# First loads in halves, wide products ahead of narrow ones, copies ahead of ropes, last sparse heads one step on: four edits to a two-layer trunk

## The chip, the cores and the metric

The kernel runs on one core of a Trainium2 chip. The metric is device time in microseconds for one execution: load of inputs from memory, both layers, output back to memory. A profile gives the engines' instructions of one execution: TensorE (PE) with its weight loads (PEld), VectorE (DVE), ScalarE (ACT), GpSimd (POOL) and SyncE (SP), which here issues most loads.

## The reference, cut to what matters

```python
for i in range(DEPTH):                       # 2 layers, x is 256 x 1024, float32
    h = x @ w_in[i]                          # 1024 x 6214: q, k, v of three mixers, indexer, gates
    (fq, fk, fv, ff_logit, sq, sk, sv, dq, dk, dv, iq, ik, iw, g) = split_cols(h)
    log_f = log_sigmoid(ff_logit + b_forget[i])
    o_fox = fox_attention(fq, fk, fv, log_f)                     # 6 heads of 64
    o_sb = stick_breaking_attention(sq, sk, sv)                  # 5 heads
    dq, dk, iq, ik = rope(dq), rope(dk), rope(iq), rope(ik)
    o_dsa = dsa_attention(dq, dk, dv, iq, ik, iw)                # 5 heads, 64 keys chosen by an indexer
    gates = sigmoid(g.reshape(b, s, 3, D_MODEL))
    merged = (gates[:, :, 0] * (o_fox @ w_up_fox[i]) + gates[:, :, 1] * (o_sb @ w_up_sb[i])
              + gates[:, :, 2] * (o_dsa @ w_up_dsa[i]))
    x = layer_norm(ALPHA * x + merged @ w_out[i], ln1_g[i], ln1_b[i])
    ffn = square(relu(x @ w_ff_in[i])) @ w_ff_out[i]             # 1024 -> 4096 -> 1024
    ple = sigmoid(x @ w_ple_gate[i]) * (p[i] @ w_ple[i])         # p is 256 x 256 in each layer
    x = layer_norm(ALPHA * x + ffn + ple, ln2_g[i], ln2_b[i])
```

## The kernel before

**Products.** Every float32 product is made of three products in the format fp32r: a tile is split into a high part (`hi`, a cast on ScalarE) and a low part (`lo`, source minus high part, on VectorE), and high by high, high by low and low by high are added up in a PSUM bank. `split` (L178) does this, its cast at L181, its subtraction at L182. `wunit` (L206) loads a piece of a weight through SyncE's queue into one of five buffers (`wr`, 128x1024 at most, `wload` L95) and splits it into `wh` and `wl`, five buffers each. TensorE then multiplies. There are eight PSUM banks in two groups of four, `pg` and `ps`.

**Tiling.** The 256 tokens are two tiles of 128. `xstat` (L242) keeps the tokens' transposed tile as the stationary side and moves the weights, 512 columns at a time; `by_tile` (L251, L256) does one token tile's high products for all units, then its low ones, and then the second tile's. `wstat` (L399) keeps the weight stationary and moves the tokens, 256 columns (L407, L409, L410). `half_T` (L320) transposes half a token tile (L217) and splits it.

**The start.** p and the weights for p's embedding (`w_ple`, first half, two pieces of 128x512) are asked for first, then x's first tile, the first gate weight of 128x1024, x's second tile. `rope` and `bf` go on GpSimd's queue, behind which GpSimd makes the masks. p is transposed (L334) and split, its products (L197) fill two banks, x is transposed and split, and `gate(0)` is made by tile (`gate` L384): 48 products for the two tiles. `ple_done` (L338) copies p's two finished banks out on ScalarE (L341). The order on each engine comes from a scheduler, apart from a few instructions held in program order by `tc.keep_in_program_order`.

**The middle.** A planner (L863 on) lets one list of products (`PRODUCTS`, L31) and one list of jobs (`JOBS`, L32) run side by side: each step issues products until 550 columns are in flight (`PACE`) and one part of each job under way. The number beside a job's name is how many steps pass before the next job may start. The sparse heads are three jobs: `dsa0`, `dsa1` (heads 1 and 2) and `dsa3` (heads 3 and 4); their scores are made at L204 into `ps` banks, and `values` (L582) casts the values product of an earlier head out of such a bank (L592, L593). `c4_done` (L544) and `c3_done` (L552) take keys and values of the sparse and stick-breaking heads out of their bank: first `do_rope` (L364, VectorE pieces L369 to L373), then the `split` into `vh` and `vl`. `fv_done` (L429) adds the forget bias and splits v.

**The gated up products.** `up` (L812) multiplies the mixers' outputs by the up weights into pairs of `pg` banks (L197, L779, L780). The gates' sigmoid (L888) must come behind all exponentials of the layer, so its bias `zero` (L885) is computed from the last head's low part; then VectorE multiplies gate and bank (L762) and the bank is free for a later pair.

**The feed forward.** `ff_in` (L936) runs 16 times, over 512 of the hidden columns each, into four `ps` banks. Each has four units of two 128-row blocks with four banks each: a wide product (L945, 512 columns: high weight by high and low part of x side by side), and right behind it a narrow one (L947, 256 columns: low weight by high x). `ff_out` (L965) then adds 48 products of 512 columns to the layer's output.

## Time and profile before

| | us |
|---|---|
| median of three runs | 885.36 |
| the runs | 884.37, 885.36, 885.51 |
| profiled execution | 885.02 |
| its span | 883.3 |
| TensorE busy | 857.3 (97%) |
| VectorE busy | 642.1 (73%) |
| ScalarE busy | 476.0 (54%) |
| granted TensorE clock, mean | 0.993 |

The span is the time between the first and last instruction that the profile holds; 1.7 us of the profiled execution lie around it. The table says that TensorE works or stands in a queue of its own work nearly all the time. A product's record lasts longer than its place in the row, since products are pipelined: the spacing from start to start is what a run of products takes for each.

### The profile page before, as it was taken

Reading aid. Unit: us, or ns where it says so; the run is one execution under the profiler, and the core shown is the slowest. Engines: PE = TensorE matmul, PEld = TensorE weight load, DVE = VectorE, ACT = ScalarE, POOL = GpSimd, SP = SyncE. Lnnn points to the kernel's source line nnn. Section 1 sums busy time; section 2 is a strip of 40 time slices with the busy share of each in tenths; the row PEclk is TensorE's granted clock in tenths of the full one; section 3 lists DMA queues with packets and bytes.
Section 4 is the critical chain, followed back from the end, with each engine's and each line's share of the span. In section 5 each row is a group of like instructions: output and inputs, shape, how many; then the busy total and the mean of one; then the engine's idle time right before and its main releaser. Section 6 shows DMA issues by size and latency. Waiting matters only on the chain. (4 is left out here: it accounts for less than half of the span.)

```text
span 883.3 us, 12940 instructions
## 1 busy us (share of the span) xinstructions
PE 857.3 (97%) x4678; PEld 733.3 (83%) x4678; DVE 642.1 (73%) x1133; ACT 476.0 (54%) x749; POOL 71.2 (8%) x138
## 2 busy tenths in 40 slices
PE   5999999999999999999999999999999999999996
PEld 4999988788888888888879989787887888888885
DVE  5479997769877666666676889968797776666665
ACT  4445657667445444444354556666843654444440
POOL 2003111100011000000000121001001010000100
PEclk9999999999999999999999999999999999999998
DMA  8555666442656556666536646554364666666731
GB/s 264 167 151 138 178 193 172 158 148 97 211 179 229 191 190 191 191 213 215 174 91 192 170 135 197 160 182 153 111 228 152 214 191 191 191 188 189 235 127 48
DMA packets 79696, 154.46 MB, mean 175 GB/s; under 512 B 10096, under 2 KB 25456, under 8 KB 79632
## 3 DMA queue, kind: packets, MB, share of 16 engines
q1 hardware_dynamic: 77952, 149.04, 54.1%
q0 software_dynamic: 1680, 4.60, 1.8%
q8 instruction: 37, 0.61, 0.3%
q14 instruction: 27, 0.22, 0.1%
HBM read 152.30 MB, written 1.05 MB: 174 GB/s over the span
## 5 line engine op out<-in xcount | busy, mean ns | idle before, releaser
L182 DVE TENSOR_TENSOR wl<-wr,wh 128x1024 fp32r<-128x1024 f32 (+5 forms) x303 | 342.8, 1142 | 178.9 <-ACT wh L181 176.6
L181 ACT CAST wh<-wr 128x1024 fp32r<-128x1024 f32 (+5 forms) x303 | 295.2, 983 | 286.0 <-PE pg L197 110.2
L197 PE MATMUL pg<-wh,t16k 128*128 128x512 f32 (+4 forms) x768 | 224.7, 367 | 0.1
L945 PE MATMUL ps<-t16k,wh 128*128 128x512 f32 x512 | 181.4, 398 | 0.0
L197 PE MATMUL pg<-wh,t2k 128*128 128x512 f32 x544 | 172.8, 394 | 1.4 <-ACT wh L181 1.2
L197 PEld LDWEIGHTS pg<-wh,t16k 128*128 128x128 f32 x768 | 140.8, 189 | 20.0 <-DVE t2k L190 0.7
L947 PE MATMUL ps<-t16k,wl 128*128 128x256 f32 x512 | 143.7, 281 | 0.0
L197 PE MATMUL pg<-wl,t16k 128*128 128x512 f32 (+4 forms) x384 | 139.6, 364 | 0.0
L197 PEld LDWEIGHTS pg<-wh,t2k 128*128 128x128 f32 x544 | 102.9, 189 | 24.0 <-ACT wh L181 1.6
L945 PEld LDWEIGHTS ps<-t16k,wh 128*128 128x128 f32 x512 | 96.2, 188 | 23.8
L197 PE MATMUL pg<-wl,t2k 128*128 128x512 f32 x272 | 106.6, 392 | 0.0
L947 PEld LDWEIGHTS ps<-t16k,wl 128*128 128x128 f32 x512 | 96.7, 189 | 0.6
L197 PEld LDWEIGHTS pg<-wl,t16k 128*128 128x128 f32 x384 | 72.5, 189 | 8.3
L197 PEld LDWEIGHTS pg<-wl,t2k 128*128 128x128 f32 x272 | 51.6, 190 | 10.7 <-DVE wl L182 0.3
L407 PE MATMUL pg<-t16k,wh 128*128 128x256 f32 x176 | 50.5, 287 | 2.4 <-DVE t16k L182 2.4
L410 PE MATMUL pg<-t16k,wl 128*128 128x256 f32 x176 | 49.8, 283 | 0.0
L409 PE MATMUL pg<-t16k,wh 128*128 128x256 f32 x176 | 49.7, 283 | 0.0
L251 PE MATMUL pg<-wh,t16k 128*128 128x512 f32 x96 | 39.0, 406 | 4.8 <-ACT t16k L181 4.8
L251 PE MATMUL pg<-wl,t16k 128*128 128x512 f32 x96 | 38.6, 403 | 0.0
L197 PE MATMUL pg<-wh,t1k 128*128 128x512 f32 x112 | 37.3, 397 | 0.0
L407 PEld LDWEIGHTS pg<-t16k,wh 128*128 128x128 f32 x176 | 33.7, 191 | 2.9 <-issue 2.8
L409 PEld LDWEIGHTS pg<-t16k,wh 128*128 128x128 f32 x176 | 33.7, 191 | 0.0
(180 smaller groups left out, 968.9 us busy)
## 6 DMA issues: line engine op xcount, KB each, us to landing
wr<-in_w_ff_in_dram SPq DMA_DIRECT2D x64, 512.0 KB, 3.8
wr<-in_w_ff_out_dram SPq DMA_DIRECT2D x64, 512.0 KB, 3.5
wr<-in_w_in_dram SPq DMA_DIRECT2D x48, 512.0 KB, 4.1
wr<-in_w_in_dram SPq DMA_DIRECT2D x32, 384.0 KB, 3.6
wr<-in_w_out_dram SPq DMA_DIRECT2D x16, 512.0 KB, 3.7
wr<-in_w_ple_gate_dram SPq DMA_DIRECT2D x16, 512.0 KB, 5.2
wr<-in_w_in_dram SPq DMA_DIRECT2D x16, 256.0 KB, 2.9
wr<-in_w_in_dram SPq DMA_DIRECT2D x8, 390.0 KB, 3.7
```

Source lines behind the costliest of these rows:

```text
L181: a = nc.scalar.copy(hi, src)
L182: b = nc.vector.tensor_sub(lo, src, hi.bitcast(F32))
L197: nc.tensor.matmul(o, l, r, start=start and i == 0, stop=stop and i == 2, skip_group_check=skip)
L251: nc.tensor.matmul(o[t][:, :n], tok(aT, u * nk + kk, t)[0], wt[i][:, kk, :], start=u + kk + i == 0, stop=False)
L407: nc.tensor.matmul(oi, hi, rh, start=kb == 0 and i % 2 == 0, stop=False, skip_group_check=True)
L409: nc.tensor.matmul(oi, hi, rl, start=False, stop=False, skip_group_check=True)
L410: nc.tensor.matmul(oi, lo, rh, start=False, stop=kb == KB - 1, skip_group_check=True)
L945: nc.tensor.matmul(pz[i], hi, x1_both[:, kb, :], start=kb == 0, stop=False, skip_group_check=True)
L947: nc.tensor.matmul(pz[i][:, 0:T], lo, x1T[0][:, kb, :], start=False, stop=kb == KB - 1, skip_group_check=True)
```

## The change

The four edits do this. First, at the start: p, then the two `w_ple` pieces, x's first tile in two halves, the first gate weight in two pieces of 128x512 and x's second tile in two halves are loaded in that order, into buffers of their own and not in `wr`'s five. Nine products of a zero tile come first on TensorE (`WARM`), with a result that nothing reads. The casts, low parts, transposes and products of the start are held in program order. p's high part is made on VectorE. `gate(0)` of the first layer is written out, with both token tiles in turn. The masks are made behind this, and `rope` and `bf` are loaded on SyncE's queue behind the gate's loads. Second, in `c4_done`, `c3_done` and `fv_done` the split comes ahead of the rope or the addition. Third, the entry of `dsa1` goes from 0 to 1 steps. Fourth, `ff_in` issues all eight wide products of a unit and then its eight narrow ones.

```diff
-JOBS = [('decay', 4), ('fox0', 2), ('fox2', 2), ('fox4', 1), ('idxT', 1), ('idx0', 3), ('idx1', 0), ('dsaT', 2), ('sb0', 2), ('sb2', 2), ('dsa0', 0), ('sb4', 2), ('dsa1', 0), ('dsa3', 4)]
+JOBS = [('decay', 4), ('fox0', 2), ('fox2', 2), ('fox4', 1), ('idxT', 1), ('idx0', 3), ('idx1', 0), ('dsaT', 2), ('sb0', 2), ('sb2', 2), ('dsa0', 0), ('sb4', 2), ('dsa1', 1), ('dsa3', 4)]
...
+WARM = 9
...
-    for k in range(2):
-        early.append(wload(wrows(w_ple, 0, k, 1, 0, 512), 1, 512))
-    nc.sync.dma_start(xs[0], x[0, 0:P, :])
-    early.append(wload(wrows(w_in, 0, 0, 2, O_G, 512), 2, 512))
-    nc.sync.dma_start(xs[1], x[0, P:T, :])
-    rope = cst.tile([P, 4, HD], F32, name="rope")
-    nc.gpsimd.dma_start(rope, rope_tab)
...
+    def first_load(w, k, c0):
+        raw = act.tile([P, 1, 512], F32, tag="t2k", name=nm("w0"), bufs=T2K)
+        nc.sync.dma_start(raw, w[0, k * P:(k + 1) * P, c0:c0 + 512].rearrange("(k p) n -> p k n", p=P))
+        return raw
...
+    def load_x(t):
+        for j in range(2):
+            nc.sync.dma_start(xs[t][:, j * 512:(j + 1) * 512], x[0, t * P:(t + 1) * P, j * 512:(j + 1) * 512])
+
+    ple_raw = [first_load(w_ple, k, 0) for k in range(2)]
+    load_x(0)
+    gate_raw = [first_load(w_in, k, O_G) for k in range(2)]
+    load_x(1)
+
+    warm = pg()
+    for _ in range(WARM):
+        nc.tensor.matmul(warm[:, 0:T], lfh[:, 0, :], lfh.rearrange("p t c -> p (t c)"), start=True, stop=True)
...
+    pin(nc.vector.tensor_copy(pT0[0], qv))
+    pin(nc.vector.tensor_sub(pT0[1], qv, pT0[0].bitcast(F32)))
+    ple_o = [(t, pg()) for t in range(2)]
+    products(ple_o, [(pT0, 0, first_unit(ple_raw[0]))], True, False)
+    w1 = first_unit(ple_raw[1])
...
     for j in range(2):
         to_xT(0, j)
+    products(ple_o, [(pT0, 1, w1)], False, True)
+    gate_o = [(t, pg()) for t in range(2)]
+    gate_w = [first_unit(raw) for raw in gate_raw]
+    blocks = [(xT, k, gate_w[k]) for k in range(2)]
+    products(gate_o[:1], blocks, True, False, KINDS[:2])
+    for j in range(2):
+        to_xT(1, j)
+    products(gate_o[:1], blocks, False, False, KINDS[2:])
+    products(gate_o[1:], blocks, True, False)
...
-        run(gate(0))
+        if l:
+            run(gate(0))
+        else:
+            for u in range(1, KB // 2):
+                wt = wunit(wrows(w_in, 0, 2 * u, 2, O_G, 512), 2, 512)
+                if u == 1:
+                    for t, o in ple_o:
+                        pe[0, t] = t2k(F32)
+                        pin(nc.scalar.copy(pe[0, t], o))
+                for t, o in gate_o:
+                    for kk in range(2):
+                        mm3(o, tok(xT, 2 * u + kk, t), tuple(v[:, kk, :] for v in wt), False,
+                            2 * u + kk == KB - 1)
...
+            nc.sync.dma_start(rope, rope_tab)
...
         def c4_done(t, o):
+            split(o[:, 320:384], vh[:, t, 768:832], vl[:, t, 768:832])
             do_rope(t, o[:, 0:256], 4, rnd[t][:, 64:320])
...
-            split(o[:, 320:384], vh[:, t, 768:832], vl[:, t, 768:832])
...
                 for kk in range(2):
-                    kb = 2 * u + kk
                     for i in range(4):
...
+                        nc.tensor.matmul(pz[i], wt[0][:, kk, i * P:(i + 1) * P], x1_both[:, 2 * u + kk, :],
+                                         start=u + kk == 0, stop=False, skip_group_check=True)
+                for kk in range(2):
+                    for i in range(4):
+                        nc.tensor.matmul(pz[i][:, 0:T], wt[1][:, kk, i * P:(i + 1) * P],
+                                         x1T[0][:, 2 * u + kk, :], start=False,
+                                         stop=2 * u + kk == KB - 1, skip_group_check=True)
```

The order of instructions shows where these edits land. On ScalarE at the start, before: the casts of p (`t2k_165`), of the two `w_ple` pieces (`wh_171`, `wh_181`), of three gate weights (`wh_213`, `wh_223`, `wh_233`), the two copies of p's banks, and then x's transposed halves (`t16k_195`).

```order
L181 CAST t2k_165<-ps_160 128x512
L181 CAST wh_171<-wr_77 128x512
L181 CAST wh_181<-wr_79 128x512
L181 CAST wh_213<-wr_82 128x1024
L181 CAST wh_223<-wr_221 128x1024
L181 CAST wh_233<-wr_231 128x1024
L341 COPY t2k_191<-pg_169 128x512
L341 COPY t2k_193<-pg_170 128x512
L181 CAST t16k_195<-ps_196 128x4x128
L181 CAST t16k_195<-ps_203 128x4x128
```

The same engine at the same place now (`wh_114` and `wh_124` are `w_ple`, `wh_151` and `wh_155` the first gate weight's halves, `wh_257` the next gate weight, `t16k_128` x).

```order
L143 CAST wh_114<-w_2_81 128x512
L143 CAST wh_124<-w_3_83 128x512
L143 CAST t16k_128<-ps_129 128x4x128
L143 CAST t16k_128<-ps_136 128x4x128
L143 CAST wh_151<-w_4_87 128x512
L143 CAST wh_155<-w_5_89 128x512
L143 CAST t16k_128<-ps_163 128x4x128
L143 CAST t16k_128<-ps_170 128x4x128
L143 CAST wh_257<-wr_255 128x1024
L458 COPY t2k_261<-pg_112 128x512
L458 COPY t2k_263<-pg_113 128x512
```

x's first half moved from ninth to third place, ahead of the gate weights, and the copies behind x's casts and one weight's cast.

On TensorE where the sparse heads' scores are made, before: the last scores of heads 1 and 2 (`ps_2115`, `ps_2116`) and, right behind, the first of heads 3 and 4 (`ps_2138`, `ps_2139`).

```order
L204 MATMUL ps_2115<-t1k_317,t2k_318 128x256
L204 MATMUL ps_2116<-t1k_317,t2k_318 128x256
L204 MATMUL ps_2115<-t1k_316,t2k_319 128x256
L204 MATMUL ps_2116<-t1k_316,t2k_319 128x256
L204 MATMUL ps_2138<-t1k_316,t2k_318 128x128
L204 MATMUL ps_2139<-t1k_316,t1k_320 128x128
L204 MATMUL ps_2138<-t1k_317,t2k_318 128x128
```

There now: behind the last scores of heads 1 and 2 (`ps_2133`, `ps_2134`) stand the products of the last gate (`pg_2094`, `pg_2095`), 24 of them, of which the first are shown.

```order
L165 MATMUL ps_2133<-t1k_335,t2k_336 128x256
L165 MATMUL ps_2134<-t1k_335,t2k_336 128x256
L165 MATMUL ps_2133<-t1k_334,t2k_337 128x256
L165 MATMUL ps_2134<-t1k_334,t2k_337 128x256
L158 MATMUL pg_2094<-wh_2157,t16k_128 128x512
L158 MATMUL pg_2094<-wl_2158,t16k_128 128x512
L158 MATMUL pg_2094<-wh_2157,t16k_128 128x512 x2
```

Behind those 24 stand six products of values (`ps_2191`) and then the scores of heads 3 and 4 (`ps_2211`, `ps_2212`):

```order
L158 MATMUL ps_2191<-t3k_2045,t16k_254 128x2x128
L158 MATMUL ps_2191<-t3k_2044,t16k_254 128x2x128
L165 MATMUL ps_2211<-t1k_334,t2k_336 128x128
L165 MATMUL ps_2212<-t1k_334,t1k_338 128x128
L165 MATMUL ps_2211<-t1k_335,t2k_336 128x128
```

So the second pair's scores moved behind the last gate's first two units.

On TensorE in the feed forward, before: each bank's wide product (`wh_2862`) with its narrow one (`wl_2863`) behind it.

```order
L945 MATMUL ps_2856<-t16k_2529,wh_2862 128x512
L947 MATMUL ps_2856<-t16k_2529,wl_2863 128x256
L945 MATMUL ps_2857<-t16k_2529,wh_2862 128x512
L947 MATMUL ps_2857<-t16k_2529,wl_2863 128x256
L945 MATMUL ps_2858<-t16k_2529,wh_2862 128x512
L947 MATMUL ps_2858<-t16k_2529,wl_2863 128x256
```

And now, at the middle of a unit: the last wide products (`wh_2880`) and the first narrow ones (`wl_2881`).

```order
L1017 MATMUL ps_2875<-t16k_2547,wh_2880 128x512
L1017 MATMUL ps_2876<-t16k_2547,wh_2880 128x512
L1017 MATMUL ps_2877<-t16k_2547,wh_2880 128x512
L1021 MATMUL ps_2874<-t16k_2547,wl_2881 128x256
L1021 MATMUL ps_2875<-t16k_2547,wl_2881 128x256
L1021 MATMUL ps_2876<-t16k_2547,wl_2881 128x256
```

The width changes twice in a unit of sixteen products, where it changed behind every one.

## Rows read from the trace of the kernel before

**Rows 1.** The page's part 1: busy time of each engine, share, instructions.

```profile
PE 857.3 (97%) x4678; PEld 733.3 (83%) x4678; DVE 642.1 (73%) x1133; ACT 476.0 (54%) x749; POOL 71.2 (8%) x138
```

**Rows 2.** One of PE's waits: us in total, times, longest.

```profile
PE ps L204 <- DVE t1k L593: 3.1, 2, 1.5
```

**Rows 3.** Timeline, first 20 us: start, duration, instruction, idle before and releaser.

```profile
6.29 1.22 PE L197 MATMUL pg<-wh,t2k 128*128 128x512 f32 x2 [1.19 <-ACT wh L181]
11.08 1.03 PE L217 MATMUL ps<-ident,x 128*128 128x128 f32 x8
16.02 1.07 ACT L341 COPY t2k<-pg 128x512 f32<-128x512 f32 x2
16.97 1.09 ACT L181 CAST t16k<-ps 128x512 fp32r<-128x512 f32 x2
17.62 0.80 PE L251 MATMUL pg<-wh,t16k 128*128 128x512 f32 x1 [4.23 <-ACT t16k L181]
```

**Rows 4.** Tile x, first 30 us: issues with durations in ns, landing.

```profile
L115 SPq DMA_DIRECT2D x<-in_x_dram x1: 432/432/432, 2.3 to 2.3; - x1
L117 SPq DMA_DIRECT2D x<-in_x_dram x1: 831/831/831, 3.2 to 3.2; - x1
DMA to landing us min/median/max: 7.5/8.3/9.1
```

**Rows 5.** Windows: PE, PEld, DVE, ACT, POOL busy; granted clock; DMA share; GB/s.

```profile
6.29:10.30 4.01, 4.01 (x10) 3.02 (x10) 1.45 (x3) 0.62 (x1) 1.08 (x5) 1.00 0.97 325
17.62:20.72 3.10, 3.10 (x7) 2.49 (x8) 2.96 (x4) 2.61 (x4) 0.00 (x0) 0.50 0.77 233
20.76:30.25 9.49, 9.49 (x43) 7.76 (x42) 1.95 (x4) 2.23 (x4) 0.00 (x0) 1.00 0.31 86
```

**Rows 6.** Timeline, 83 to 89.5 us, at the shared key's values.

```profile
86.78 0.81 DVE L182 TENSOR_TENSOR wl<-wr,wh 128x640 fp32r<-128x640 f32 x1
87.51 0.21 DVE L182 TENSOR_TENSOR t16k<-pg,t16k 128x64 fp32r<-128x64 f32 x1
87.87 0.36 PE L407 MATMUL pg<-t16k,wh 128*128 128x256 f32 x1 [1.14 <-DVE t16k L182]
```

**Rows 7.** Timeline, 172 to 177 us, first layer's sparse heads.

```profile
173.36 2.36 DVE L182 TENSOR_TENSOR wl<-wr,wh 128x1024 fp32r<-128x1024 f32 x2 [0.39 <-ACT wh L181]
175.75 0.77 DVE L593 TENSOR_TENSOR t1k<-ps,t1k 64x256 fp32r<-64x256 f32 x2
176.24 0.32 PE L204 MATMUL ps<-t1k,t2k 64*128 64x128 f32 x1 [1.54 <-DVE t1k L593]
```

**Rows 8.** Window behind them, columns as in Rows 5.

```profile
177.73:181.14 3.41, 3.41 (x9) 2.65 (x9) 3.10 (x20) 2.39 (x13) 0.00 (x0) 0.50 0.79 254
```

**Rows 9.** Timeline, 190 to 201 us, last head's low part to the gated banks.

```profile
194.31 1.01 DVE L182 TENSOR_TENSOR t3k<-ps,t3k 128x384 fp32r<-128x384 f32 x2
195.50 1.05 ACT L181 CAST wh<-wr 128x1024 fp32r<-128x1024 f32 x1 [1.59 <-issue]
198.62 0.69 DVE L762 TENSOR_TENSOR t2k<-pg,t2k 128x512 f32<-128x512 f32 x1 [0.81 <-ACT t2k L888]
200.28 0.50 PE L779 MATMUL pg<-wh,t1k 128*128 128x512 f32 x1
```

**Rows 10.** Timeline of PE, second layer's first feed forward group.

```profile
708.66 0.39 PE L945 MATMUL ps<-t16k,wh 128*128 128x512 f32 x1
...
719.96 0.40 PE L197 MATMUL pg<-wh,t2k 128*128 128x512 f32 x1
```

**Rows 11.** Chain of waits ahead of it: start, us, piece.

```profile
697.88 10.94 PE pg L197 x48
```

**Rows 12.** Timeline of PE, a run of narrow products.

```profile
38.79 0.28 PE L407 MATMUL pg<-t16k,wh 128*128 128x256 f32 x1
...
41.18 0.28 PE L410 MATMUL pg<-t16k,wl 128*128 128x256 f32 x1
```

**Rows 13.** Weight loads by line: busy us, mean ns, idle before.

```profile
L410 PEld LDWEIGHTS pg<-t16k,wl 128*128 128x128 f32 x176 | 33.7, 191 | 0.0
```

More of the change, by code (lines that the diff above doesn't have):

```diff
@@ new lines, in pin, with first_unit, products @@
+    def pin(ins):
+        if pinned[0]:
+            tc.keep_in_program_order(ins)
+    def first_unit(raw):
+        hi = wp.tile([P, 1, 512], F32R, tag="wh", name=nm("wh"), bufs=WH)
+        lo = wp.tile([P, 1, 512], F32R, tag="wl", name=nm("wl"), bufs=WH)
+        split(raw, hi, lo)
+        return hi, lo
+    KINDS = ((0, 0), (1, 0), (0, 1))
+    def products(outs, blocks, start, stop, kinds=KINDS):
+        for i, (a, b) in enumerate(kinds):
+            for n, (aT, kb, w) in enumerate(blocks):
+                for t, o in outs:
+                    pin(nc.tensor.matmul(o, tok(aT, kb, t)[a], w[b][:, 0, :], start=start and i + n == 0,
+                                         stop=stop and i == len(kinds) - 1 and n == len(blocks) - 1))
@@ L358, in hybrid_trunk @@
+    cmask = cst.tile([P, 2], F32, name="cmask")
+    nc.gpsimd.memset(cmask[:, 0:1], 0.0)
+    nc.gpsimd.memset(cmask[:, 1:2], 1.0)
+    for b in range(0, P, 32):
+        nc.gpsimd.memset(cmask[b:b + 8, 0:1], 1.0)
+        nc.gpsimd.memset(cmask[b:b + 8, 1:2], 0.0)
+    sel = cst.tile([P, 3, T], F32R, name="sel")
+    cT = cst.tile([P, T], F32R, name="cT")
+    rope = cst.tile([P, 4, HD], F32, name="rope")
+    bf = cst.tile([P, L, H_FOX], F32, name="bf")
     for l in range(L):
@@ L394, in second_T @@
                 to_xT(1, j)
-        run(gate(0))
+        if l:
[11 more added lines that the diff above has]
+                            2 * u + kk == KB - 1)
+            pinned[0] = 0
+            for t, o in gate_o:
+                gates[0, t] = t2k(F32)
+                nc.scalar.copy(gates[0, t], o)
+            nc.sync.dma_start(rope, rope_tab)
+            nc.sync.dma_start(bf, bass.AP(tensor=b_forget.tensor, offset=b_forget.offset,
+                                          ap=[[0, P], [H_FOX, L], [1, H_FOX]]))
         def wstat(n, unit, done):
```

124 lines of the change are left out of this document (56 added, 68 removed).

## The prediction

> **What bounds the kernel now.** I read the busy shares first, then TensorE's waits, then the timeline at each long wait, then the rate of the product runs. TensorE is busy for 857.3 of the 883.3 us of the span [rows 1] and idle for 26.0. No other engine is above 73%, so the time is TensorE's count of products at their spacing, plus the places where it stands or runs slowly. A gain must therefore be a wait removed on TensorE, a stretch at the low clock shortened, or a smaller spacing.
>
> Three kinds of place are touched. The start: the first product comes at 6.29 after 1.19 of idle time, and the first gate product at 17.62 after 4.23 of it, released by a ScalarE cast of the transposed x that stood behind weight casts and two copies [rows 3]. Ten products take the 4.01 us from 6.29 (0.40 each), although the clock row says 1.00 there; seven take 3.10 us from 17.62 at a granted clock of 0.50, the level of 1.2 GHz (0.44 each); from 20.76 the clock is 1.00, 2.4 GHz, and the gate ends at 30.25 [rows 5]. The sparse heads: two waits of 1.5, one in each layer [rows 2], the first followed by 3.4 us at 0.50 [rows 7, 8]. The feed forward: no wait at all, but 32 pairs of a wide and a narrow product take 719.96 − 708.66 = 11.30 us [rows 10], 0.3531 a pair.
>
> **The change part by part. A, the start.** I replay it by the order of instructions and these rows. The first product loses one ScalarE cast ahead of it (p's copy goes to VectorE): 6.29 − 0.5 = 5.8. Its six products take 1.4 at the high spacing, 2.6 at the low one: 7.2 to 8.4. The first x tile landed 7.5 after its issue at 2.3, so at 9.8, the second at 3.2 + 9.1 = 12.3 [rows 4]. In halves they move the same bytes, but the 128 KB rope table no longer shares the queues; at the 325 GB/s of that stretch [rows 5] this is 0.4, so 9.4 and 11.9. Eight transposes take 1.03 [rows 3], most of them before the second half is there: about 10.0. The second ple product's six fill to 11.4, or 12.6 at the low spacing. ScalarE casts the two x halves (1.09 for two [rows 3]), then the two gate weights of half size (about 0.55 each): free at about 12.6, so four high products end at 13.6 or 14.4. The second tile's transposes, landed at 11.9, follow to 14.5, its casts to 15.2 or 15.6; the eight products behind them end near 16.5. Then unit 1's whole cast, 1.05 [rows 9], and its low part on VectorE, 2.36 / 2 = 1.18 [rows 7], come behind the x casts: 15.2 + 2.3 = 17.5, so TensorE waits some 0.8 after the first two products. The 34 left at 0.228 (10.94 for 48 [rows 11]) take 7.8: the gate ends near 25.0 instead of 30.25, a gain of 5.3. Two copies are still ahead of unit 2's cast on ScalarE, 1.07 together [rows 3], but TensorE has unit 1's products, 2.7 us of them, to cover that. The nine warm-up products run on zeros before p has landed: they cost nothing, and whether they bring the high clock decides between the two columns above. If the low spacing lasts until the second x tile, ten products cost 0.2 more each, of which part falls into waits for loads: gain 4. Were everything ready, 60 products at 0.228 and 2.1 of transposes from 5.8 would end at 21.6: gain 8.6, the upper bound. I take 5.3, from 4 to 8.
>
> The loads of rope and b_forget move onto SyncE's queue behind the gate's, and the next weights wait behind them. Their cover is the gate's own products, about 8 us from 17 on. If it isn't enough, the first v product is late by at most the 0.4 of those bytes. I cost this at nothing.
>
> **B, copies ahead of ropes.** At 87.87 TensorE had waited 1.14 for a bank whose last reader is a 64-column low part of 0.21 at 87.51; ahead of it on VectorE stood a weight low part of 0.81 and the rope's pieces [rows 6]. With the copies first, the last reader is the rope's last small piece, at about the time the low part could begin: 0.2 of the wait goes, for each layer; the weight's 0.81 stays. Sum 0.4, from 0 (the small piece is as late) to 0.7. For v of the forgetting heads nothing waits on y soon: nothing.
>
> **C, the last sparse heads one step on.** The scores wait 1.54 at 176.24 because the bank's reader, at 175.75, stood behind 2.36 us of weight low parts [rows 7]. One step on puts 24 gate products, 5.5 us at 0.228, between the two pairs' scores, as the order of the sparse heads shows: the reader is long done. The wait goes in both layers, 3.1 together. In the first layer the window behind it held 9 products in 3.41 us at 0.50 [rows 8]; at 0.228 nine take 2.05, so 1.4 more. The price is at the other end. The gates' sigmoid comes behind the last head's low part, and the third pair of up banks is free only when the first gated products are done. Before, the last low part ended at 195.32 and the first gated multiply at 199.31, with one cast of 1.05 between [rows 9]: 3.0 without that cast; a head's low part, a cast taken as long and three transposes come ahead of that, 0.5 + 0.5 + 0.4 = 1.4 by 1.01 for two [rows 9] and 1.03 for eight [rows 3]. So 4.4 us from the last transposes, against 16 products, 3.4 us, that TensorE now has there (28 before). New wait: about 1.1 a layer, from 0 (other work lies between) to 2.5 (weight casts queue ahead as that one did). Sum of C: 3.1 + 1.4 − 2.2 = 2.3, plus 0.3 for the short wait at 200.28 that is part of the new one [rows 9]: 2.6, from −0.2 to 4.8.
>
> **D, wide products ahead of narrow ones.** Wide products alone go at 10.94 / 48 = 0.2279 [rows 11], narrow ones alone at (41.18 − 38.79) / 20 = 0.1195 [rows 12]: together 0.3474 against 0.3531 for a pair in turn. The 0.0057 is the price of changing width back and forth. Of 512 pairs, 64 units of eight, one change per unit remains: 448 × 0.0057 = 2.6. From 0 (the price isn't one of changing) to 3.3. The low weights are wanted eight products later, so no engine has less time than before.
>
> The narrow run rests on weight loads that overlap. A load is recorded at 191 ns [rows 13], longer than the 119.5 between narrow products that each have their own, so in rows 12 two loads are under way at once. By the Trainium skill ("TensorE: Matmul & The Clock Gate", Part 3: Packing small matmuls — row/col tiling, The mechanism) a weight load overlaps a product in flight only where they take other rows of the array; all products here take all 128 rows. By that rule the run would go at the pace of the loads, which is the last rival below; rows 12 disagree with it.
>
> **Sum:** 5.3 + 0.4 + 2.6 + 2.6 = 10.9. The profiled execution took 885.02, a span of 883.3 and 1.7 around it; it gives 874.1. The median of the three runs is 885.36, so 874.5.
>
> **The rivals.** (1) The start is bound by loads: the halves land no earlier and the clock is low until the second x tile, so that only about 2 of 5.3 come: 877.8. For it speaks that x landed 7.5 to 9.1 after its issue with the queues at 97% [rows 4, 5]; against it, that the 4.23 of idle time was ended by ScalarE and not by a load [rows 3]. (2) The wait moves from the sparse heads to the gated banks in full and the clock falls there: C becomes −2, 879.9 less what is left of the short waits, about 879. Rows 9 speak for it: even before, TensorE had little to spare there. (3) Everything fits: warm clock from the first product, A 8, C 4: 870.5. (4) The change does what it says, but TensorE hands it back: with products closer together, loads or VectorE's low parts are late later on, and 9 to 11 us go again: 884 to 886. VectorE at 73% and loads at about half of the queues' time speak against it. (5) Slower, by weight loads laid bare: a narrow run goes at 0.191 a product instead of 0.1195. Each unit has seven such steps, 64 × 7 × 0.0715 = 32 on top of the forecast's sum: 874.5 + 32, about 906. It decides from a narrow spacing of 0.1195 + 10.9 / 448 = 0.144 on: there the change as a whole brings nothing. Rows 12 speak against it, with the same kind of stationary and moving tiles, though in a place where three products share two weights.
>
> **How the numbers follow.** Forecast 874.5: 0.60. Rival 1: 0.13; rival 2: 0.10; rival 3: 0.09; rival 4: 0.05, of which 0.03 within 0.2% (1.8 us, about what a measurement of this kernel can tell from no change) and 0.02 slower by more; rival 5: 0.03. So faster 0.92, same 0.03, slower 0.05. The range takes in the forecast with its bounds and rivals 1 to 3, 0.92 together: 870 to 880.
>
> **What the profile of the changed kernel would show.** A: first gate products at about 13, the first v product at 24 to 26.5, no wait of over 1.5 us on x's cast, and a spacing of 0.23 from before 13 on. B: the wait at the shared key's values down by 0.2. C: no wait of 1.5 at the third pair's scores, and a new one of about 1 ahead of the third pair of up banks. D: eight wide products in 1.83 and eight narrow ones in 0.95, no low weight waited for. It would be wrong if narrow products in a run show more than 0.125 (D gone), if the first v product comes after 28, or if the wait ahead of the gated banks is over 3.

## The result, and the profile after

The changed kernel takes 873.69 us (median of four runs, 872.19 to 874.91) against 885.43 for the kernel before: a ratio of 0.9867, interval 0.9847 to 0.9886. Forecast were 874.5 and a range of 870 to 880. The profiled execution took 872.19, the shortest of the four, with a span of 870.5: 12.8 less than the span before, where the sum had 10.9.

First the page's part 1 and TensorE's waits after the change (us in total, times, longest):

```profile
PE 852.0 (98%) x4687; PEld 731.7 (84%) x4687; DVE 642.2 (74%) x1135; ACT 472.2 (54%) x749; POOL 70.2 (8%) x136
```

```profile
PE pg L480 <- DVE t L427: 2.9, 2, 1.5
PE pg L852 <- DVE t2k L835: 2.1, 2, 1.1
PE pg L135 <- DVE lfh L111: 1.3, 1, 1.3
```

The wait at the sparse heads' scores [rows 2] is gone, a wait of 1.1 ahead of the gated up banks (L852) is new, once in each layer, and the wait at the shared key's values (L480) is longer than it was at 1.14 [rows 6]. TensorE's wait on x's cast ahead of the gate, 4.23 [rows 3], no longer stands among the long ones.

The time at which TensorE comes to the same place in both traces, worked out from its timeline, tells where the 12.8 us lie (the first v product is the first of 390 columns, right behind the gate):

| place | before | after | gained since the last place |
|---|---|---|---|
| first v product, layer 1 | 30.25 | 23.05 | 7.20 |
| last shared product of the middle (L407), layer 1 | 105.05 | 98.12 | −0.27 |
| last gated up product (L779), layer 1 | 215.48 | 206.20 | 2.35 |
| first v product, layer 2 | 462.73 | 451.81 | 1.64 |
| last shared product, layer 2 | 537.62 | 526.92 | −0.22 |
| last gated up product, layer 2 | 646.41 | 635.01 | 0.70 |
| end of the span | 883.31 | 870.49 | 1.42 |

The start gave 7.2, the copies ahead of ropes took 0.5, the sparse heads gave 3.05. The two feed forward layers, with what stands around them, gave 3.06; of that, 2.9 is theirs, as the fourth part below shows.

**The start.** Timeline of the changed kernel, ScalarE and TensorE, and the landing of tile x in the first 30 us:

```profile
8.20 1.16 ACT L143 CAST t16k<-ps 128x512 fp32r<-128x512 f32 x2 [1.21 <-PE ps L178]
9.25 1.14 ACT L143 CAST wh<-w 128x512 fp32r<-128x512 f32 x2
9.97 1.45 PE L328 MATMUL pg<-wh,t16k 128*128 128x512 f32 x4
15.22 0.50 PE L158 MATMUL pg<-wl,t16k 128*128 128x512 f32 x1 [0.31 <-DVE wl L144]
```

```profile
DMA to landing us min/median/max: 5.1/5.6/6.1
```

x's first casts start at 8.20 where they started at 16.97, and the first gate product stands at 9.97 where it stood at 17.62 [rows 3]. x's halves land 5.1 to 6.1 after their issue, the first tile whole at 8.03 and the second at 10.72; whole tiles took 7.5 to 9.1 [rows 4].

**The shared key's values.** GpSimd, VectorE and TensorE around the wait of layer 1:

```profile
78.84 0.73 POOL L430 TENSOR_TENSOR t2k<-t,t 128x256 f32<-128x256 f32 x1 [0.25 <-DVE t L427]
78.95 1.30 DVE L144 TENSOR_TENSOR wl<-wr,wh 128x640 fp32r<-128x640 f32 x1
79.51 0.84 POOL L623 CAST t16k<-t16k 128x64 fp32r<-128x64 f32 x1
80.40 0.18 DVE L427 TENSOR_TENSOR t<-pg,rope 128x32 f32<-128x32 f32 x1
80.66 0.46 POOL L432 TENSOR_TENSOR t1k<-t,t 128x128 f32<-128x128 f32 x1 [0.32 <-DVE t L427]
80.73 0.36 PE L480 MATMUL pg<-t16k,wh 128*128 128x256 f32 x1 [1.42 <-DVE t L427]
```

The value's low part is early now, but the bank's last reader is the rope's last piece at 80.40, and ahead of it stands a weight's low part that took 1.30; before, the low part of that size ahead of the last reader took 0.81 [rows 6]. All of the 1.30 lies beside GpSimd's work. GpSimd's rope product (L430) had begun 0.11 ahead of the low part, the two lie side by side for 0.62, and the low part ends 0.68 behind the product. The copy of the value (L623), which the early split now releases at this point, began while the low part was under way; it takes 0.84 and ends 0.10 behind it.

**The gated banks.** ScalarE and TensorE in layer 1:

```profile
187.85 1.28 ACT L961 ACT_TABLE_LOAD   x1
189.15 0.72 ACT L961 ACTIVATE t2k<-t2k,small 128x512 f32<-128x512 f32 x1
```

```profile
190.65 0.50 PE L852 MATMUL pg<-wh,t1k 128*128 128x512 f32 x1 [1.05 <-DVE t2k L835]
```

The chain of sigmoid, gated multiply and bank is as it was [rows 9]; TensorE now comes to its end 1.05 early.

**The feed forward.** TensorE in the second layer's second group, the one that stands in [rows 10], from its start into its third unit, at its end, and at the start of the next:

```profile
696.92 1.98 PE L1017 MATMUL ps<-t16k,wh 128*128 128x512 f32 x8
698.73 1.11 PE L1021 MATMUL ps<-t16k,wl 128*128 128x256 f32 x8
699.69 2.00 PE L1017 MATMUL ps<-t16k,wh 128*128 128x512 f32 x8
701.53 1.12 PE L1021 MATMUL ps<-t16k,wl 128*128 128x256 f32 x8
702.48 0.40 PE L1017 MATMUL ps<-t16k,wh 128*128 128x512 f32 x1
...
708.07 0.40 PE L158 MATMUL pg<-wh,t2k 128*128 128x512 f32 x1
...
718.97 0.39 PE L1017 MATMUL ps<-t16k,wh 128*128 128x512 f32 x1
```

The 64 products take 708.07 − 696.92 = 11.15 (11.30 before, [rows 10]), and the 48 behind them 10.90 (10.94 before, [rows 11]), though the edit doesn't touch these. From start to start, the first eight wide products take 1.81, and the eight that come behind a narrow run take 1.84.

### The profile page after: what moved, and what is told of

It is laid out like the page before. It is cut to its first block, busy times and chain, and to the rows that moved or that the text cites. A ratio compares the mean times of both kernels' runs of the same rounds, so it can differ in the third digit from the quotient of the medians.

```text
span 870.5 us, 12949 instructions
## 1 busy us (share of the span) xinstructions
PE 852.0 (98%) x4687; PEld 731.7 (84%) x4687; DVE 642.2 (74%) x1135; ACT 472.2 (54%) x749; POOL 70.2 (8%) x136
## 3 DMA queue, kind: packets, MB, share of 16 engines
HBM read 152.30 MB, written 1.05 MB: 176 GB/s over the span
## 4 chain that ended last, share of the span: by engine, by line
PE 45%; DVE 3%; issue 1%; ACT 1%; DMA 0%; POOL 0%; POOLq 0%; DVEq 0%
PE pg L158 24%; PE ps L1017 7%; PE ps L1021 4%; PE pg L211 2%; PE pg L216 1%; PE pg L480 1%; PE pg L483 1%; PE pg L482 1%; DVE wl L144 1%; PE ps L165 1%; PE ps L178 1%; PE ps L158 1%; DMA wr<-in_w_in_dram 0%; DVE x L261 0%; ACT wh L143 0%
## 5 line engine op out<-in xcount | busy, mean ns | idle before, releaser
L144 DVE TENSOR_TENSOR wl<-wr,wh 128x1024 fp32r<-128x1024 f32 (+4 forms) x300 | 340.9, 1148 | 169.0 <-ACT wh L143 167.8
L143 ACT CAST wh<-wr 128x1024 fp32r<-128x1024 f32 (+4 forms) x300 | 292.9, 986 | 292.9 <-PE pg L158 109.2
L158 PE MATMUL pg<-wh,t16k 128*128 128x512 f32 (+4 forms) x792 | 231.1, 366 | 0.1
L158 PE MATMUL pg<-wh,t2k 128*128 128x512 f32 x536 | 168.1, 390 | 0.2 <-ACT t2k L143 0.2
L158 PE MATMUL pg<-wl,t16k 128*128 128x512 f32 (+4 forms) x396 | 143.6, 363 | 0.3 <-DVE wl L144 0.3
L1017 PE MATMUL ps<-t16k,wh 128*128 128x512 f32 x512 | 127.8, 391 | 0.0
L1021 PEld LDWEIGHTS ps<-t16k,wl 128*128 128x128 f32 x512 | 69.8, 190 | 5.0
L1021 PE MATMUL ps<-t16k,wl 128*128 128x256 f32 x512 | 71.4, 282 | 0.0
L480 PE MATMUL pg<-t16k,wh 128*128 128x256 f32 x176 | 50.5, 287 | 2.9 <-DVE t L427 2.9
L480 PEld LDWEIGHTS pg<-t16k,wh 128*128 128x128 f32 x176 | 33.6, 191 | 3.4 <-issue 3.3
L483 PEld LDWEIGHTS pg<-t16k,wl 128*128 128x128 f32 x176 | 33.7, 191 | 0.0
L211 PE MATMUL pg<-wh,t16k 128*128 128x512 f32 x80 | 31.5, 394 | 0.6 <-ACT t16k L143 0.6
```

The costliest lines, as they stand in the source:

```text
L143: a = nc.scalar.copy(hi, src)
L144: b = nc.vector.tensor_sub(lo, src, hi.bitcast(F32))
L158: nc.tensor.matmul(o, l, r, start=start and i == 0, stop=stop and i == 2, skip_group_check=skip)
L211: nc.tensor.matmul(o[t][:, :n], tok(aT, u * nk + kk, t)[0], wt[i][:, kk, :], start=u + kk + i == 0, stop=False)
L480: nc.tensor.matmul(oi, hi, rh, start=kb == 0 and i % 2 == 0, stop=False, skip_group_check=True)
L483: nc.tensor.matmul(oi, lo, rh, start=False, stop=kb == KB - 1, skip_group_check=True)
```

## The experiments

Each kernel is the changed one with one thing edited, unless it says more. Spans stand against the changed kernel's 870.5; since the start differs from one execution to the next (below), each step is read from the place behind it.

### The sparse heads' entry back

```diff
-('dsa1', 1)
+('dsa1', 0)
```

> The changed kernel with the second sparse job's entry back at 0 steps. Theory (the heads' wait was exchanged for a smaller one at the gated banks): two waits of about 1.5 us return at the third pair's scores, the waits of 1.05 ahead of the gated up banks fall below 0.3, and in the first layer the clock is low again for about 3.4 us; span 870.5 + 2.4 + 0.7 = 873.6. Rival (the waits went because the start is earlier and the weights' low parts are done sooner, not because of the step): the waits do not return, span within 0.5 of 870.5.

Measured: 878.97 us (877.24 to 880.77), ratio to before 0.9914 (0.9890 to 0.9938), span 878.4. TensorE's wait at the scores, and windows behind it in both layers (busy times of PE, PEld, DVE, ACT, POOL, then the granted clock, DMA share, GB/s):

```profile
PE ps L165 <- DVE t1k L666: 3.1, 2, 1.5
```

```profile
171.28:177.40 6.12, 6.12 (x22) 4.97 (x23) 5.09 (x29) 3.73 (x16) 0.00 (x0) 0.50 0.88 215
604.00:607.93 3.93, 3.91 (x18) 3.16 (x18) 3.12 (x21) 2.50 (x11) 0.00 (x0) 0.57 0.97 283
```

Both waits return at 1.54 and the wait ahead of the gated banks is gone: the exchange of one wait for a smaller one is as the theory has it, and the rival falls. The size was wrong. 2.0 of the 7.9 us that the span grew are the start; the heads cost 3.6 in layer 1 and 2.3 in layer 2. Of these 5.9 only 3.1 − 2.1 = 1.0 is waits. The rest is products at the granted clock of 0.50, 1.2 GHz: 6.1 us of them in layer 1 and most of 3.9 in layer 2, where the kernel before had 3.4 and none. So in four instances the same wait of 1.54 was followed by no low clock once, by 3.4 us of it twice, and by over 6 once. What the edit is worth is 1 us of waits and, in the two executions that were profiled without it, some 2 and 5 of clock.

### Copies behind the ropes again

```diff
-            split(o[:, 320:384], vh[:, t, 768:832], vl[:, t, 768:832])
             do_rope(t, o[:, 0:256], 4, rnd[t][:, 64:320])
             do_rope(t, o[:, 256:320], 1, rnk[t][:, 128:256], dup=2)
             nc.gpsimd.tensor_copy(rnd[t][:, 320:384], rnk[t][:, 128:192])
+            split(o[:, 320:384], vh[:, t, 768:832], vl[:, t, 768:832])
```

The same for the two other places.

> The changed kernel with the copies of values behind the ropes and the addition again, in all three places. Theory (the edit made the ropes' pieces the last readers of the bank, behind two weights' low parts of 1.30 us): the wait of 1.42 and 1.46 at the shared key's values goes back to about 1.15, span 870.5 - 0.5 = 870.0. Rival (the wait grew because the start's shift brought the weights' low parts earlier): the wait stays at 1.4, span 870.5 within 0.2.

Measured: 872.91 us (871.74 to 873.29), ratio 0.9843 (0.9826 to 0.9861), span 871.2. TensorE's wait there:

```profile
PE pg L480 <- DVE t16k L144: 2.4, 2, 1.2
```

The waits are 1.15 and 1.21 again, released by the low part as before. The span is 0.7 longer, not 0.5 shorter, because this execution's first v product came at 24.20 instead of 23.05; behind it the kernel gains 0.45. That the edit costs 0.5 in two layers and not the start's shift holds. The reason that I put down was half wrong, since I took the 1.30 for two low parts. It is one, and here it takes 0.81 again:

```profile
80.74 0.81 DVE L144 TENSOR_TENSOR wl<-wr,wh 128x640 fp32r<-128x640 f32 x1
80.89 0.97 POOL L432 TENSOR_TENSOR t1k<-t,t 128x128 f32<-128x128 f32 x1 [0.75 <-DVE t L427]
```

In this order VectorE does the rope's small pieces first, GpSimd's product of 128x256 is over, and its next one, of 128x128, begins 0.15 behind the low part. It is now GpSimd's product that takes 0.97, where it takes 0.46 in the changed kernel. So it is in both layers of the four kernels with the copies behind the ropes. In both layers of the ten with the copies ahead the low part takes 1.30 or 1.35: the product of 128x256 began 0.05 to 0.12 ahead of it, they overlap by 0.61 to 0.68, and the low part ends 0.68 behind the product. So the 0.5 goes with the rope's product that was already under way, and not with the copy of the value. Whether the other two places of the edit matter was not tried apart, nor a kernel with that product alone put later. The Trainium skill ("GPSIMD Engine Reference", 1. Specifications) says that GpSimd shares its way to the on-chip memory with VectorE and that they contend where a VectorE instruction has two inputs there, as this subtraction has (`wr` and `wh`). The rows agree, with the one that came first keeping its time and the other one losing it.

### Narrow products back behind their wide ones, and in fours

The first kernel has the old order of `ff_in`. The second issues four wide and four narrow products in turn:

```diff
                 for kk in range(2):
                     for i in range(4):
                         nc.tensor.matmul(pz[i], wt[0][:, kk, i * P:(i + 1) * P], x1_both[:, 2 * u + kk, :],
...
-                for kk in range(2):
                     for i in range(4):
                         nc.tensor.matmul(pz[i][:, 0:T], wt[1][:, kk, i * P:(i + 1) * P],
```

> The changed kernel with each bank's narrow product right behind its wide one again. Theory (every change of width costs about 5 ns): a feed forward group of 64 goes from 11.146 back to 11.290, 2.3 us in 16 groups, and the 48 products after it stay at 10.907, since they have no change of width: span 872.8. Rival (the order of widths also decides how the runs of products behind it go): these return to 10.943 as well, 0.6 more: span 873.4.

> The changed kernel with four wide and four narrow products in turn in the feed forward, so two changes of width in eight products instead of two in sixteen. Theory (a price for each change of width): a group of 64 goes from 11.146 to 11.146 + 0.144 x 4/28 = 11.167. Rival (the wide and the narrow run as such are cheaper, by what else their operands do, and four in a row are too short for it): a group nearer to 11.29.

Measured: 875.96 us (874.94 to 876.74), ratio 0.9879 (0.9861 to 0.9897), span 873.2 for the old order; 874.90 in one run, span 873.2, for the fours, whose first v product came 1.5 later. From the timelines, the means over 16 groups; a group's time is the same within a nanosecond in all 16 of a kernel:

| order of widths | 64 products of a group | 48 wide ones behind | wide to wide | wide to narrow | narrow to narrow | narrow to wide |
|---|---|---|---|---|---|---|
| in turn (before, and undone) | 11.290 | 10.943 | – | 0.2360 | – | 0.1168 |
| in fours | 11.200 | 10.927 | 0.2326 | 0.2287 | 0.1184 | 0.1186 |
| in eights (the change) | 11.146 | 10.907 | 0.2296 | 0.2267 | 0.1189 | 0.1200 |

TensorE in fours, the same group, for its two ends:

```profile
699.09 1.07 PE L1017 MATMUL ps<-t16k,wh 128*128 128x512 f32 x4
...
710.29 0.40 PE L158 MATMUL pg<-wh,t2k 128*128 128x512 f32 x1
...
721.22 0.39 PE L1017 MATMUL ps<-t16k,wh 128*128 128x512 f32 x1
```

The edit is worth 16 × 0.144 = 2.3 in the groups and 16 × 0.036 = 0.6 behind them, 2.9 together, and undoing it takes both back. A price for each change of width falls: fours should have been 11.167 and are 11.200, which is not nearer to 11.29 either, as the rival has it; and the step from wide to narrow is the cheaper one of its row, not the dearer one. The means of the table hide where the time lies. Place by place in the same timelines, a wide product that has long had wide ones ahead of it goes at 0.2267 in all of these kernels, and in a run of eight the narrow ones settle at 0.120. Behind a narrow run of eight the next five wide products are dearer, by 0.028 together, and the sixth is back at 0.2267; this is the 1.84 against 1.81 above. Behind a group in turn the next ten are dearer, by 0.063, behind a group in fours the next nine, by 0.047, and so the 48 wide ones behind a group are dearer too. The first narrow product of a run of eight gives back 0.007. At 0.2267 and 0.120 a group of 32 and 32 would take 11.093: in turn costs 0.197 above that, in fours 0.107, in eights 0.053. So a return to wide products costs something for up to ten of them, and the edit makes such returns rarer. By what mechanism, these runs don't show.

### The warm-up: none, and more

```diff
-WARM = 9
+WARM = 0
```

```diff
-WARM = 9
+WARM = 11
...
+    for _ in range(4):
+        pin(nc.tensor.matmul(warm[:, 0:T], lfh[:, 0, :], lfh.rearrange("p t c -> p (t c)"), start=True, stop=True))
     qv = q.rearrange("p (k t) -> p k t", t=T)
```

> The changed kernel without the nine warm-up products on zeros. Theory (they bring the high clock forward to the first ple products): the low spacing of 0.43 lasts some 3 to 4 us longer, eight to ten products at 0.2 more, and the first v product comes at 24.5 to 25 instead of 23.05: span 872. Rival (the first products wait for loads and casts anyway, and a slower one fits into the waits): the first v product comes at most 0.4 later, span below 871.

> The changed kernel with eleven warm-up products at the start and four more between p's transposes and the first ple product, so that TensorE stands nowhere for over 0.3 from 1.26 to the first ple product. Four profiles of one and the same start had the rise to the high spacing at about 6.4 twice, at 8.8 and at 10.4. Theory (the idle time between the warm-up products and the first ple product decides it): the high spacing is there by 6.4 in the profile, first v product at 23.1 or sooner, and the runs lie within 1 us of each other below 872.5. Rival (the rise falls where it falls, whatever TensorE does in these few us): times spread over 872 to 875 as before.

Measured: 873.94 us without (873.79 to 874.73, ratio 0.9860, 0.9840 to 0.9880), span 872.1; 872.40 with more (872.12 to 872.73, ratio 0.9843, 0.9825 to 0.9860), span 870.7. The same first four ple products, without and with more:

```profile
5.69 2.04 PE L328 MATMUL pg<-wh,t2k 128*128 128x512 f32 x4 [0.88 <-DVE t2k L338]
```

```profile
5.88 1.21 PE L328 MATMUL pg<-wh,t2k 128*128 128x512 f32 x4 [0.40 <-ACT wh L143]
```

Without, the first v product comes at 24.62, as expected, but that alone proves nothing: kernels with nine warm-up products and no other edit ahead of that place differ as much among themselves. The time from the first ple product to x's first transposition, which stands right behind the sixth, tells the clock. Beside it stands the time at which the trace's own record of the granted clock begins, at 1.00; ahead of that the trace has none, and the window view prints 1.00 for want of one, as it does in the first line of [rows 5]:

| kernel | warm-up | six ple products | clock record begins | first v product |
|---|---|---|---|---|
| the changed one | 9 | 1.80 | 5.0 | 23.05 |
| narrow ones back | 9 | 1.80 | 5.1 | 22.97 |
| copies back | 9 | 2.70 | 9.0 | 24.20 |
| heads' entry back | 9 | 2.72 | 10.4 | 25.06 |
| in fours | 9 | 2.73 | 9.3 | 24.59 |
| none | 0 | 2.69 | 10.6 | 24.62 |
| more | 11 + 4 | 1.85 | 5.1 | 23.35 |

Six products in 2.7 us are at the spacing of the stretch granted 0.50 [rows 5]. With nine warm-up products TensorE stands for 0.25 or more ahead of p's transposes and for 0.88 or more behind them, and three of these five executions start at the low spacing, as the one without any. So do all four of the next experiment, which keep the nine (2.70 each): seven of nine in all, one of them with gaps of 0.19 and 0.88, no longer than the 0.25 and 0.88 of the two at the high spacing. With 15, which fill the first gap and the second but for 0.4, this execution and both of the last experiment (1.82 and 1.93) are at or near the high one. Whether it is the filled gaps or only the six products more was not tried apart. The four runs lie within 0.6 us of each other; those of the changed kernel lie within 2.7. What the theory forecast came near, as far as four runs and three profiles go (the first v product at 23.35 and not by 23.1, one run above 872.5), and the warm-up as it was made pays only now and then: its four runs have nearly the median of the four without, 873.69 against 873.94.

### What set the start: loads or ScalarE's order

Rope and b_forget on GpSimd's queue at the start again; x in whole tiles; the next gate weight's cast and the copies ahead of x's second tile; and ScalarE's whole old order:

```diff
+    nc.gpsimd.dma_start(rope, rope_tab)
+    nc.gpsimd.dma_start(bf, bass.AP(tensor=b_forget.tensor, offset=b_forget.offset,
...
-            nc.sync.dma_start(rope, rope_tab)
...
```

```diff
-        for j in range(2):
-            nc.sync.dma_start(xs[t][:, j * 512:(j + 1) * 512], x[0, t * P:(t + 1) * P, j * 512:(j + 1) * 512])
+        nc.sync.dma_start(xs[t], x[0, t * P:(t + 1) * P, :])
```

```diff
+    w_u1 = wunit(wrows(w_in, 0, 2, 2, O_G, 512), 2, 512)
+    for t, o in ple_o:
+        pe[0, t] = t2k(F32)
+        pin(nc.scalar.copy(pe[0, t], o))
     for j in range(2):
         to_xT(1, j)
...
```

```diff
-    for j in range(2):
-        to_xT(0, j)
     products(ple_o, [(pT0, 1, w1)], False, True)
...
     gate_w = [first_unit(raw) for raw in gate_raw]
+    w_u = [None] + [wunit(wrows(w_in, 0, 2 * u, 2, O_G, 512), 2, 512) for u in (1, 2)]
+    for t, o in ple_o:
+        pe[0, t] = t2k(F32)
+        pin(nc.scalar.copy(pe[0, t], o))
+    for j in range(2):
+        to_xT(0, j)
...
```

> The changed kernel with rope and b_forget asked for at the start again, on GpSimd's queue, all else as changed. Theory (x landed 1.7 sooner than before because these two transfers, small pieces among them, no longer lie in front of it): x's first tile lands at 9.3 to 9.8 instead of 8.03, its second near 12.2 instead of 10.72, and the first gate product comes 1.3 to 1.7 later. Rival (the halves and the gate weight's pieces make the difference): landings within 0.4 of 8.03 and 10.72.

> The changed kernel with each x tile loaded whole. Theory (not the halves but what else is asked for at that time set the landing): the first tile lands whole within 0.4 of 8.03, and only the first four transposes come later, by 0.5 to 0.7, which falls into later waits: first v product within 0.5 at the same state of the clock. Rival (halves land sooner): the tile lands at 9 or later.

> The changed kernel with gate unit 1's cast and the two copies of p's banks ahead of the casts of x's second tile on ScalarE, as they stood before. Theory (the order on ScalarE was the cause of most of the 4.2 us in which TensorE stood before the gate): x's casts come behind unit 1's landing (12.07) and 2.1 of work, near 14.2 instead of 11.89, and TensorE stands about 2.3 there, of which the 0.7 wait for unit 1's low part is given back: first v product 1.5 to 2.0 later. Rival (loads set the start): at most 0.5 later.

> The changed kernel with ScalarE's order at the start as it was: both gate weights' halves, units 1 and 2 and the two copies of p's banks are cast ahead of x's first tile. Theory (this order was the cause of TensorE's 4.2 us ahead of the gate, and the loads were not): unit 2 lands near 13.4, so x's first cast comes near 15.6 instead of 8.2 and the first gate product at 16.3 instead of 9.97; some of it falls into a fuller run behind it, first v product at 27 to 29, span 874.5 to 877. Rival (clock and loads set the start, as a later cast of the second tile alone cost nothing): first v product before 25.5.

| kernel | us | ratio to before (interval) | x's tiles landed | first gate product | first v product |
|---|---|---|---|---|---|
| the changed one | 873.69 | 0.9867 (0.9847 to 0.9886) | 8.03, 10.72 | 9.97 | 23.05 |
| rope early | 875.21 | 0.9874 (0.9850 to 0.9898) | 9.41, 12.11 | 11.69 | 24.78 |
| x whole | 874.00 | 0.9861 (0.9838 to 0.9883) | 8.15, 10.78 | 11.58 | 24.62 |
| second tile behind the copies | 873.45 | 0.9854 (0.9832 to 0.9877) | 8.70, 11.37 | 11.64 | 24.59 |
| ScalarE's old order | 879.35 | 0.9917 (0.9886 to 0.9948) | – | 16.02 | 30.34 |

The first three began at the low spacing, so they are to be held against the executions that did so too: first v product at 24.20 to 25.06. None of the three is later than that. Rope and b_forget in front cost x's landing 0.7 to 1.8 us, 9.41 where the twelve kernels without them have 7.6 to 8.7, but at the low clock TensorE is still busy with ple products when x lands. At the high one this was not seen; there TensorE's weight load for the transposition of x's second half already waits 0.15 for its landing in the changed kernel. The second half lands no sooner than a whole tile, 8.03 against 8.15; the first lands at 7.34, which at the low spacing gains nothing. A late cast of the second tile alone costs nothing, since TensorE finds unit 1's products of the first tile ready in that place; my expectation of 1.5 to 2.0 fell. ScalarE's old order decides. TensorE and ScalarE of this last kernel:

```profile
15.37 1.09 ACT L143 CAST t16k<-ps 128x512 fp32r<-128x512 f32 x2
```

```profile
16.02 2.08 PE L328 MATMUL pg<-wh,t16k 128*128 128x512 f32 x4 [3.90 <-ACT t16k L143]
```

With halves, late rope and warm-up all in place, TensorE stands for 3.90 again, released by the cast of x, the next four products go at the low spacing, and the first v product is back at 30.34, where it was at 30.25 [rows 5] and where the changed start at the low spacing has 24.20 to 25.06; that is later than the 27 to 29 that I expected. Without the order of the casts nothing is left of what the edit brought at the start. That this order alone, with none of the rest, would bring it all was not tried.

### Two attempts at a better version

Both have the longer warm-up and the copies behind the ropes. The first also loads the sigmoid's table early, the second takes the bias of the gates from the last softmax.

```diff
                 nc.vector.reciprocal(mn[:, 4:6], mn[:, 2:4])
+                norm[0] = mn[:, 4:5]
...
+        nc.scalar.activation(small(1), norm[0], AF.Sigmoid)
         zero = small(1)
```

```diff
                 nc.vector.reciprocal(mn[:, 4:6], mn[:, 2:4])
+                last[0] = mn[:, 4:5]
...
-                last[0] = pT[1].bitcast(F32)[:, i, 0:1]
```

> The changed kernel with the longer warm-up, the copies behind the ropes again, and a sigmoid of one column behind the last exponential of a layer, which makes ScalarE load the sigmoid's table there instead of ahead of the gates. Theory (the table's 1.28 us lie on the chain that ends at the gated banks, 0.75 of it alone): the wait of 1.05 ahead of the gated banks falls to 0.3 to 0.5 in each layer, the wait at the shared key's values to 1.15, span 870.5 - 1.2 - 0.5 + 0.2 = 869.0, times near 870.8. Rival (another cast or the last low part ends last there): the wait stays above 0.9.

> As the one before, but with the bias of the gates' sigmoid taken from the last softmax's reciprocal instead of from the low part of the last transposed head, and without the extra sigmoid: sigmoids may start some 5 us sooner. Theory (the chain to the gated banks is then short enough): no wait ahead of these banks, 2.1 gained in two layers, if the values' casts behind the sigmoids on ScalarE aren't late by as much: span 868.4. Rival (the sigmoids, 0.7 each, push the last head's casts back, and TensorE waits for these): a wait of 1 to 3 us in each layer at the values or the third pair, span 870 to 873.

Measured: 871.25 us (871.13 to 871.65), ratio 0.9826 (0.9806 to 0.9847), span 869.5 for the first; 872.54 (872.41 to 872.77), ratio 0.9840 (0.9820 to 0.9861), span 870.9 for the second. The first kernel's table load and first sigmoid, and its wait there:

```profile
180.41 1.28 ACT L960 ACT_TABLE_LOAD   x1
181.71 0.20 ACT L960 ACTIVATE small<-small 128x1 f32<-128x1 f32 x1
188.78 0.72 ACT L965 ACTIVATE t2k<-t2k,small 128x512 f32<-128x512 f32 x1 [0.74 <-DVE small L962]
```

```profile
PE pg L855 <- DVE t2k L838: 1.1, 2, 0.6
```

And TensorE's waits in the second kernel at the last head's values and behind:

```profile
PE ps L158 <- ACT t3k L143: 1.6, 2, 0.8
PE pg L158 <- DVE wl L144: 1.1, 3, 0.4
```

The table was on the chain: with it out of the way, the gates' sigmoid waits for its bias only, and TensorE's wait falls from 1.05 to 0.58 in each layer, somewhat less far than the 0.3 to 0.5 expected. Sigmoids that start earlier still do away with that wait and make others of the same size, since the last head's cast stands behind them on ScalarE: the second rival holds. The first kernel is the best one here, 2.4 us below the changed kernel by medians (3.6 by the ratios to the kernel before, which was measured anew beside each) and with no run above that kernel's lowest.

## Why the prediction was right, step by step

The time, the range and the likeliest case were right; three terms were too small, one had the wrong sign, and the errors went partly against each other.

**A, the start: forecast 5.3, measured 7.2 in the profile, 5.2 to 7.3 in five executions of this start.** The mechanism, ScalarE's order, is shown by the kernel with the old order. Three steps of the working were off. x was put at 9.4 and 11.9 and landed at 8.03 and 10.72, and the first gate product at about 13 and came at 9.97: I counted only the rope table's bytes, 0.4, where the rope and b_forget transfers cost 0.7 to 1.8. The working's last step, 17.5 and 7.8, gives 25.3 and not 25.0, so a gain of 5.0. And the high column and the low one of the working are both real, but which one comes is settled anew in each execution; the five have 1.80 or 2.7 us for the first six products. The rival with a bound by loads has not come: at the low spacing nothing was lost with x landing later.

**B, the copies: forecast a gain of 0.4, measured a loss of 0.5.** The step that failed is "the last reader is the rope's last small piece, at about the time the low part could begin". The piece is the last reader, but I replayed VectorE in the order and with the durations of before. With the split first, the weight's low part comes ahead of the rope's small pieces and right behind the start of GpSimd's rope product, and takes 0.5 longer beside it: without this 0.5 the wait of 1.42 would be 0.92, and the 0.2 of the forecast would have come. This cause is argued from the rows of fourteen kernels, which leave no exception, and was not tried by itself.

**C, the heads: forecast 2.6, measured 3.05 (2.35 and 0.70).** Both waits went, the new one was put at 1.1 and is 1.05. The 0.3 for a short wait at 200.28 is not in [rows 9], whose line shows no idle time. The 1.4 for the clock in layer 1 is not a constant of the kernel: with the edit undone the clock cost some 5 us in two layers, with the same waits. In rival 2 the terms as written give 879.1, not 879.9.

**D, the widths: forecast 2.6, measured 2.9.** The spacings of runs, taken from other places of the kernel, were good to 0.002 for the wide ones and 0.001 for the narrow ones. The reason, one price for each change, was wrong, and the 0.6 in the runs behind was not seen. The 0.2279 of [rows 11] holds the dearer products behind a group in turn, where the settled spacing is 0.2267; and what stays in eights is not one change of 0.0057 a unit but some 0.013, a quarter of the 0.053. These two errors go against each other, so that 2.6 came near 2.3 in the groups is in part luck. The narrow run goes at 0.119, so the rival with loads laid bare has not come. The Trainium skill's rule on weight loads that stood beside it ("TensorE: Matmul & The Clock Gate", Part 3: Packing small matmuls — row/col tiling, The mechanism) doesn't hold for this run: its loads are recorded at 0.190 on all 128 rows, longer than the 0.119 from one product to the next.

The sum of the four was 10.9; 12.8 came in the profiled execution, 11.7 by medians. By the table of the start, that execution was one with a high spacing from the first products on, which is worth 1.2 to 2.0. That the median came within 0.8 of the forecast is therefore in part luck.

## What to carry to other kernels

Where an engine feeds the busiest one from a queue in order, ask first which of its instructions is wanted next, and only then how soon its inputs land: here the order of a dozen casts was worth 5 to 7 us, and halves of loads nothing that could be seen. An instruction moved ahead of another moves the other one back: replay both with what is queued on that engine, and with what another engine already has under way, before taking a gain. A mean spacing can hide that only the first few products of a run are dear: read it place by place. A wait taken off TensorE may be worth more than its length, for the clock that it would have cost, and that part changes from execution to execution: read several.

## What the runs showed of the hardware

- A wide product's spacing on TensorE, with no wait anywhere, is 0.2267 in a long wide run and on the mean 0.2360 in turn with narrow ones, 0.2326 in fours, 0.2296 in eights. Behind narrow products the next wide ones are dearer: five of them by 0.028 together behind a run of eight, ten by 0.063 behind a group in turn. A group's time is the same within a nanosecond in all 16.
- One wait of 1.54 us ahead of the same products was followed by nothing, by 3.4 us, or by more than 6 us at the granted clock of 0.50.
- Whether the first six ple products take 1.8 or 2.7 us differed between executions of the same start, as long as TensorE stood about a microsecond ahead of them: with nine warm-up products seven of nine took 2.7. With six more of these products, which fill the gaps, they took 1.82 to 1.93 in three of three.
- A subtraction of 128x640 on VectorE takes 0.81 to 0.83 in all places but one; there, begun 0.05 to 0.12 behind a GpSimd product of 128x256, it takes 1.30 and 1.35 and ends 0.68 behind that product. Where it begins 0.15 ahead of a GpSimd product of 128x128 it keeps its 0.81, and the product takes 0.97 instead of 0.46. In the same way a subtraction of 128x768, in one place of each layer of all fourteen kernels, takes 1.63 instead of 0.95 with a GpSimd product of 128x320 under way for the first 0.82 of it.
- With a table of 128 KB and a load of 6 KB asked for on another queue ahead of x and beside it, x's first tile landed at 9.41, in one execution, and at 7.6 to 8.7 in the twelve kernels without; 128 KB at the stretch's 325 GB/s [rows 5] would be 0.4.
